# Condition steps moved into the experts' second product, low weight halves made two tiles ahead, and further reorderings in a two-block transformer kernel

## The chip, the cores and the metric

The kernel runs on one core of one Trainium2 chip. The metric is device time in microseconds: 1697.27 us is the median of three runs of the kernel before (1693.96 to 1698.69). The profile is of one further execution.

## The reference, cut to what matters

One sequence of 256 positions with 1024 channels, all in float32, goes through two blocks. The first has an attention layer of two kinds side by side, then a layer of 16384 experts. The second has two layers, each a mixer and a gated feed-forward; the vectors that scale and shift its norms come from a condition `c` through a large product, here called the condition product.

```python
# first block
h = rms_norm(x, attn_norm)
sb_q, sb_k, sb_v, cq, ckv, k_pe = split(h @ w_in)
sb  = stick_breaking_attention(sb_q, sb_k, sb_v)              # 8 heads of 64
q   = rms_norm(rms_norm(cq, cq_norm) @ w_uq, q_norm)          # then rope on 32 of 96
kv  = rms_norm(ckv, ckv_norm) @ w_ukv                         # keys and values
k   = rms_norm(concat(k_nope, k_pe), k_norm)                  # then rope
mla = chunk_causal_softmax_attention(q, k, v)
x   = x + concat(rms_norm(sb), rms_norm(mla)) @ w_o
x   = x + peer_ffn(rms_norm(x))          # sum over chosen experts of g * gelu(x.u) * v
# second block: shift, scale and gate come from silu(c) @ ada
layer 0: x += g * (concat(rmsnorm(diff_attend(..)), fourier(..)) @ w_out); x += g * swiglu(..)
layer 1: x += g * conformer(..)   # product, 31-tap depthwise conv, layernorm, silu, product
         x += g * swiglu(..)      # (silu(h @ w1) * (h @ w3)) @ w2, width 2816
```

## The kernel before, in words

Every weight is used as a high and a low half in a reduced float format, and three products (high by high, high by low of the activations, low by high) stand for one float32 product. A weight tile is 128 by 1024 numbers and costs TensorE 24 matmuls of 256 columns. `_load` issues its DMA on SyncE, `_hi` makes the high half on ScalarE (a tile called `wh`), `_lo` the low half on VectorE (`a<-a,wh`). `next_w` (L629) hands out tile i: it loads into a ring of four raw slots as earlier tiles are given back, then emits `_hi` up to tile i+2 and `_lo` up to tile i+`los`. All engines take their instructions in the order in which they were emitted, so the place of an `_hi` or `_lo` in its engine's row of work says what it waits behind.

The first mixer makes the queries and the compressed keys, then four value tiles (`for i in range(4)`, L896) between which it writes the normalised `cq` (`wq`) and `ckv` (`wk`) and runs steps of `rope`, which builds the sine and cosine tables. After this the key's rope is applied, and a planner (`weave`) mixes the main line of products (`main`, steps `s`: a query and a key tile, `k`: keys, `v`: values, `m`: queries of the second kind) with the tasks of the attention heads.

The experts' second product (L1368) is a loop over 128 keys, one weight tile each. Between the tiles the condition product advances by steps of `ada`, a VectorE pass over a 128 by 1024 tile with an accumulated sum: three steps in every five keys for layer 0. The 48 steps of layer 1 are taken later, in the differential mixer (`diff`) and in the feed-forward of layer 0.

`diff` mixes six heads and a Fourier part, whose results form eight tiles that are multiplied by the output weight in the order `ORDER`. Each feed-forward (`ffn`, L1720) is a loop over 22 slices f: a tile of w1, a tile of w3, and the w2 tile of the slice before. `Pre` lets its first `raws` tiles use the activations before normalisation, with the scale applied afterwards (`praw`, `pcol` on VectorE), while `pre.write()` writes the normalised ones. In the layer-0 feed-forward each f also takes two `ada` steps and builds four diagonal matrices for the convolution on ScalarE.

The conformer convolves with taps divided over TensorE (`PE_TAPS`), GpSimd (`POOL_TAPS`) and VectorE; then come the sums for the layer norm, the Silu, and the last product.

Of the kernel before, what the change touches and what calls it, by code (L numbers as in the profile page):

```python
# [2 lines left out]

# [12 lines left out]
AF = mybir.ActivationFunctionType  # L16
# [4 lines left out]
P = 128  # L21
# [16 lines left out]
PE_TAPS = (8, 9, 9, 9, 9, 9, 14, 15)  # L38
# [35 lines left out]
ORDER = (6, 0, 1, 2, 3, 7, 4, 5)  # L74
# [372 lines left out]
class Net:  # L447
# [394 lines left out]
    def first_mixer(self, ctx):  # L842
# [49 lines left out]
        next(wq)  # L892
# [20 lines left out]
        self.copy(kr[64:QR], kpe[64:QR], scale=self.vec("k_norm")[64:QR])  # L913
        for o, i in ((slice(64, 80), slice(96, QR)), (slice(96, QR), slice(64, 80))):
            nc.vector.tensor_tensor(kt[o], kr[i], self.sinE[i], op=ALU.mult)
        nc.vector.tensor_tensor(kr[64:QR], kr[64:QR], self.cosE[64:QR], op=ALU.mult)
        for o in (slice(64, 80), slice(96, QR)):
            nc.vector.tensor_tensor(kr[o], kr[o], kt[o], op=ALU.add)
# [16 lines left out]

        def main():
# [233 lines left out]
    def peer(self, ctx):  # L1170
# [186 lines left out]
        cg = None  # L1357
        for i in range(NKEYS):
# [18 lines left out]
            if i == 6:  # L1377
                for v in range(2):
                    self.act(cs[v], cs[v], AF.Silu)
                self.table(AF.Exp)  # L1380
                ada = self.ada(0, [self.t(sp, [P, D], tag=f"adaw{i}") for i in range(2)], cs, self.arena(0, D))
            if i > 8 and i % 5 < 3:
                next(ada, None)
# [13 lines left out]
    def ada(self, layer, ws, cs, junk=None):  # L1397

        nc = self.nc
        at = 0  # L1400

        def load():
            nonlocal at
            if at < 48:
                nc.sync.dma_start(ws[at % len(ws)], self.a["ada"][layer, at])
                at += 1
# [4 lines left out]
        for m in range(48):  # L1411
# [41 lines left out]
    def diff(self, ctx):  # L1453
# [13 lines left out]
        self.steps = self.ada(1, [ar(14 * U + i * D, D) for i in range(3)], [ar(5120, D)])  # L1467
# [95 lines left out]
        def main():  # L1563
# [61 lines left out]
        self.pre = Pre(self, self.xT, *self.modulation(2, 0, 1), 0, ar(12 * U, 3, 2, T), ar(12 * U + 1536, T), ar(8 * U, KD, T), AF.Silu, 6)  # L1625
# [92 lines left out]
    def ffn(self, ctx, layer):  # L1718
# [4 lines left out]
        self.los = 1  # L1723
        acc = [self.bank("at") for _ in range(4)]
        cs = []
        for f in range(NF + 1):
# [24 lines left out]
            for _ in range((2, 3, 0, 0)[min(f, 3)]):  # L1751
                pre.write()
# [29 lines left out]
    def conformer(self, ctx):  # L1782
# [22 lines left out]
        def conv_pool(j):  # L1805
            p, u, n = taps[j % 2], us[j % 3], POOL_TAPS[j]
            for i in range(n):
                k = TAPS - n + i
                kw = {"bias": self.vec("dw_b", j)} if i == 0 else {}
                nc.scalar.activation(p[:, i], u[:, k:k + T], AF.Identity if i == 0 else AF.Copy, scale=dw(j, k), **kw)  # L1810
            while n > 1:
# [108 lines left out]
        nc.gpsimd.tensor_tensor(pt[j], pt[j], c, op=ALU.subtract)  # L1920
# [4 lines left out]
        while self.w_lo < self.w_used + 2:  # L1925
            self._lo()
# [5 lines left out]
        self.copy(d, sums[0], scale=1.0 / D)  # L1932
# [4 lines left out]
        for k in range(2):  # L1937
            nc.vector.tensor_tensor(y[:, k], y[:, k], dp, op=ALU.subtract)
        for k in range(2, KD, 2):
            nc.gpsimd.tensor_tensor(y[:, k], y[:, k], d, op=ALU.subtract)  # L1940

        def normal(k):
            if k > 1 and k % 2 == 1:
# [11 lines left out]
        for k in range(KD):  # L1955
            if k < KD - 2:
                self.acc_t(acc, self.next_w(), hh[:, k], hl[:, k], k == 0)
            if k == KD // 2:
                self.table(AF.Exp)
                self.pre = Pre(self, self.xT, *self.modulation(4, 1, 1), 0, ar(13 * U, 3, 2, T), ar(13 * U + 1536, T), ar(7 * U, KD, T), AF.Silu, 6)  # L1960
# [195 lines left out]
```

## Time and profile before

| | us |
|---|---|
| median of the runs | 1697.27 |
| the profiled execution | 1694.07 |
| its span | 1692.3 |
| TensorE busy | 1636.0 (97%) |
| VectorE busy | 1333.6 (79%) |
| ScalarE busy | 1009.4 (60%) |
| GpSimd busy | 325.5 (19%) |

In the profile PE is TensorE, DVE VectorE, ACT ScalarE, POOL GpSimd and SP SyncE. Almost all PE rows have one line number and almost all others another, since helpers record them; so groups are told apart by the names of their tiles and by their time.

### The profile page before, as it was taken

The numbers are of one execution on the slowest core, as the hardware profiler recorded it, in microseconds if no ns is written. First come the engines' busy times: TensorE is split into PE (matmuls) and PEld (weight loads), VectorE is DVE, ScalarE is ACT, GpSimd is POOL, SyncE is SP. The second block draws the span as 40 slices with busy tenths as digits, with TensorE's granted clock in tenths as the row PEclk, the third lists the DMA queues.
The fourth block names the chain that finished last, engine by engine and source line by source line (L and its number), as shares of the span: only waits on it lengthen the run. The fifth ranks groups of instructions, "written<-read, shape, count | busy, mean of one in ns | idle before, by whom it ended". The sixth has DMA issues, their size and how long they took to land.

```text
span 1692.3 us, 33577 instructions
## 1 busy us (share of the span) xinstructions
PE 1636.0 (97%) x12986; PEld 1574.0 (93%) x12986; DVE 1333.6 (79%) x2379; ACT 1009.4 (60%) x1935; POOL 325.5 (19%) x198
## 2 busy tenths in 40 slices
PE   7999999999999999999999999998999989899998
PEld 6878999999999999999999997878999989789997
DVE  7787999977778867878788789976877799885555
ACT  5875554578777756444454564565655677564444
POOL 1020789900000000000000024311000057310000
PEclk9999999999999999999999999999999999999999
DMA  7323455544444456677887753323888732245553
GB/s 218 117 88 120 157 178 180 180 161 162 163 164 162 162 197 233 236 248 235 320 291 275 249 195 119 133 100 123 306 305 300 257 113 100 75 152 187 186 187 125
DMA packets 88110, 315.66 MB, mean 187 GB/s; under 512 B 10000, under 2 KB 11024, under 8 KB 87696
## 3 DMA queue, kind: packets, MB, share of 16 engines
q1 hardware_dynamic: 87952, 313.51, 54.7%
q8 instruction: 104, 1.70, 0.4%
q14 instruction: 54, 0.44, 0.1%
HBM read 312.03 MB, written 1.05 MB: 185 GB/s over the span
## 4 chain that ended last, share of the span: by engine, by line
PE 71%; DVE 14%; ACT 6%; DMA 4%; POOL 2%; issue 2%; SPq 0%; DVEq 0%; ACTq 0%; POOLq 0%
PE mm L179 41%; PE at L179 30%; DVE a L209 10%; ACT a L209 3%; POOL a L209 2%; DMA a<-in_peer_v_dram 2%; ACT wh L209 2%; DMA a<-in_w_dram 1%; DMA a<-in_peer_u_dram 1%; DVE praw L209 1%; DVE dmx L209 1%; DVE xT L209 1%; DVE adaw L209 0%; DVE gb L209 0%; DVE de L209 0%
## 5 line engine op out<-in xcount | busy, mean ns | idle before, releaser
L209 ACT ACTIVATE wh<-a 128x1024 fp32r<-128x1024 f32 (+3 forms) x491 | 515.1, 1053 | 262.6 <-DMA a<-in_w_dram 120.4
L179 PE MATMUL mm<-a,wh 128*128 128x256 f32 (+3 forms) x4736 | 655.1, 287 | 13.5 <-ACT wh L209 6.8
L209 DVE TENSOR_TENSOR a<-a,wh 128x1024 fp32r<-128x1024 f32 (+2 forms) x436 | 533.3, 1230 | 121.3 <-ACT wh L209 115.9
L179 PEld LDWEIGHTS mm<-a,wh 128*128 128x128 f32 (+1 forms) x4736 | 600.7, 189 | 26.6 <-ACT wh L209 7.6
L179 PE MATMUL mm<-a,a 128*128 128x256 f32 (+5 forms) x2608 | 409.3, 295 | 12.3 <-DVE a L209 7.9
L179 PEld LDWEIGHTS mm<-a,a 128*128 128x128 f32 (+1 forms) x2608 | 354.6, 190 | 24.0 <-DVE a L209 6.5
L179 PE MATMUL at<-a,wh 128*128 128x256 f32 x2152 | 283.3, 282 | 7.3 <-DVE a L209 4.9
L179 PEld LDWEIGHTS at<-a,wh 128*128 128x128 f32 x2152 | 268.5, 190 | 9.3 <-DVE a L209 5.7
L209 POOL TENSOR_TENSOR a<-a 128x256 f32<-128x256 f32 (+4 forms) x44 | 71.5, 1626 | 885.5 <-ACT a L209 860.0
L179 PE MATMUL at<-a,a 128*128 128x256 f32 (+6 forms) x1288 | 210.5, 297 | 2.3 <-DVE a L209 2.3
L179 PEld LDWEIGHTS at<-a,a 128*128 128x128 f32 (+2 forms) x1288 | 171.5, 190 | 16.6 <-issue 10.5
L209 ACT ACTIVATE a<-a 128x256 fp32r<-128x256 f32 (+7 forms) x220 | 99.1, 460 | 109.2 <-DVE a L209 87.1
L209 POOL TENSOR_TENSOR a<-a,a 128x256 f32<-128x256 f32 (+5 forms) x62 | 80.3, 1300 | 427.6 <-ACT a L209 336.4
L209 POOL TENSOR_TENSOR a<-a,wh 128x1024 fp32r<-128x1024 f32 x54 | 147.1, 2745 | 17.1 <-ACT wh L209 16.8
L209 DVE TENSOR_TENSOR a<-a,a 128x256 fp32r<-128x256 f32 (+7 forms) x189 | 111.7, 592 | 22.3 <-ACT a L209 17.5
L209 ACT ACTIVATE a<-mm 128x256 f32<-128x256 f32 (+29 forms) x173 | 60.2, 352 | 95.8 <-PE mm L179 95.7
L179 PE MATMUL at<-fgh,wh 128*128 128x256 f32 x352 | 86.3, 282 | 2.2 <-ACT wh L209 2.2
L179 PE MATMUL at<-fgl,wh 128*128 128x256 f32 x352 | 86.1, 282 | 0.0
L209 ACT ACTIVATE oh<-oh,rest 128x128 f16<-128x128 f16 x256 | 81.1, 398 | 0.0
L209 DVE TENSOR_TENSOR fs<-fs,mm 128x256 f32<-128x256 f32 x38 | 16.0, 422 | 76.3 <-PE mm L179 76.3
L209 DVE TENSOR_TENSOR a<-a,at 128x204 f32<-128x204 f32 (+54 forms) x115 | 36.6, 355 | 48.7 <-PE at L179 41.8
L179 PEld LDWEIGHTS at<-fgh,wh 128*128 128x128 f32 x352 | 66.4, 189 | 2.7 <-ACT wh L209 2.7
(163 smaller groups left out, 1565.4 us busy)
## 6 DMA issues: line engine op xcount, KB each, us to landing
a<-in_w_dram SPq DMA_DIRECT2D x132, 512.0 KB, 3.5
a<-in_peer_u_dram SPq DMA_DIRECT2D x128, 512.0 KB, 3.3
a<-in_peer_v_dram SPq DMA_DIRECT2D x128, 512.0 KB, 4.0
adaw<-in_ada_dram SPq DMA_DIRECT2D x48, 512.0 KB, 4.4
a<-in_ada_dram SPq DMA_DIRECT2D x48, 512.0 KB, 4.9
a<-in_pw_dram SPq DMA_DIRECT2D x24, 512.0 KB, 3.3
a<-in_w_pq_dram SPq DMA_DIRECT2D x16, 512.0 KB, 3.2
a<-in_ev_qkf_dram SPq DMA_DIRECT2D x14, 512.0 KB, 3.6
```

Of the source, the lines that this page charges most:

```text
L179: return self.engine.matmul(out, w, x, **kw)
L209: return f(*args, **kw)
```

## The change

There are five places.

In the first mixer `ckv` is written before `cq`, the table steps run one per value tile, and the rest of them with the key's rope (`key_rope`) goes into the first `qk` of the main line; the DMA that spreads the rotated key to all heads moves to the `k` step. In `diff` the tile order changes and eight `ada` steps go away. They are taken in the experts' second product, which now does 1.03 steps per key for 32 keys and 0.515 per key after. In both feed-forward layers `raws` goes from 6 to 10, `pre.write()` is spread one per slice, and `los` goes from 1 to 2. In the conformer one tap moves from TensorE to VectorE, one subtraction on GpSimd moves ahead of the tree sum, and the work around the layer norm is reordered: one `_lo` ahead and one behind instead of two ahead.

```diff
-PE_TAPS = (8, 9, 9, 9, 9, 9, 14, 15)
+PE_TAPS = (8, 9, 9, 9, 9, 9, 14, 14)
-ORDER = (6, 0, 1, 2, 3, 7, 4, 5)
+ORDER = (6, 7, 0, 1, 2, 3, 4, 5)
+FIRSTMODS = 8
@@ first mixer
-        next(wq)
         nk.mm()
...
-                if kk == 0:
-                    next(rope, None)
-            next(wq, None)
-            next(wk, None)
+            if i < 2:
+                next(wk, None)
+            if i > 0:
+                next(wq, None)
             next(rope, None)
-        for _ in rope:
-            pass
...
+        def key_rope():
+            for _ in rope:
+                yield
+            self.copy(kr[64:QR], kpe[64:QR], scale=self.vec("k_norm")[64:QR])
...
                 if kind == "s":
-                    yield from qk(p)
-                    if p == 0:
-                        nc.sync.dma_start(km[64:QR], self.bc(kr[64:QR], HEADS))
+                    for _ in qk(p):
+                        if p == 0:
+                            next(turned, None)
+                        yield
...
                 if kind == "k":
+                    for _ in turned:
+                        pass
+                    nc.sync.dma_start(km[64:QR], self.bc(kr[64:QR], HEADS))
@@ the experts' second product
-            if i > 8 and i % 5 < 3:
-                next(ada, None)
+            if i > 8:
+                while given < 1.03 * min(i - 8, 32) + 0.515 * max(i - 40, 0):
+                    next(ada, None)
+                    given += 1
@@ diff
-        self.steps = self.ada(1, [ar(14 * U + i * D, D) for i in range(3)], [ar(5120, D)])
+        self.steps = self.ada(1, [ar(14 * U + i * D, D) for i in range(3)], [ar(5120, D)], begin=FIRSTMODS)
...
-            for n, _ in enumerate(values(1, "mm")):
-                if 1 < n < 7:
-                    next(steps, None)
-                yield
+            yield from values(1, "mm")
             for i in range(2):
                 self.copy(fT[:, i], self.tile_t(lh, ll))
-                next(steps, None)
                 yield
-            next(steps, None)
...
-        self.pre = Pre(self, self.xT, *self.modulation(2, 0, 1), 0, ar(12 * U, 3, 2, T), ar(12 * U + 1536, T), ar(8 * U, KD, T), AF.Silu, 6)
+        self.pre = Pre(self, self.xT, *self.modulation(2, 0, 1), 0, ar(12 * U, 3, 2, T), ar(12 * U + 1536, T), ar(8 * U, KD, T), AF.Silu, 10)
@@ ffn
-        self.los = 1
+        self.los = 2
...
-            for _ in range((2, 3, 0, 0)[min(f, 3)]):
+            if f < 5:
                 pre.write()
@@ conformer
-        nc.gpsimd.tensor_tensor(pt[j], pt[j], c, op=ALU.subtract)
...
-        while self.w_lo < self.w_used + 2:
-            self._lo()
+        self._lo()
...
-        for k in range(2):
-            nc.vector.tensor_tensor(y[:, k], y[:, k], dp, op=ALU.subtract)
-        for k in range(2, KD, 2):
-            nc.gpsimd.tensor_tensor(y[:, k], y[:, k], d, op=ALU.subtract)
+        nc.vector.tensor_tensor(y[:, 0], y[:, 0], dp, op=ALU.subtract)
+        self._lo()
```

How the instructions move is shown at three places. The first is ScalarE in the first mixer, behind the fourth value tile. `wh` is a weight's high half; the 32-row instructions are the sines; `a_98<-at` are the two copies of the values. Before:

```order
L209 ACTIVATE wh_446<-a_81 128x1024
L209 ACTIVATE a_156<-a_152 128x64
L209 ACT_TABLE_LOAD
L209 ACTIVATE a_104<-a_152 32x64
L209 ACTIVATE a_103<-a_156,a_159 32x64
L209 ACTIVATE a_104<-a_152 32x64
L209 ACTIVATE a_103<-a_156,a_159 32x64
L209 ACTIVATE wh_471<-a_86 128x1024
```

And in the changed kernel, where `wh_482` is the first key tile, `wh_520` the next one, and `a_105` the last piece of `cq`:

```order
L211 ACTIVATE a_105<-a_95 128x256
L211 ACTIVATE a_156<-a_152 128x64
L211 ACT_TABLE_LOAD
L211 ACTIVATE wh_482<-a_90 128x1024
L211 ACTIVATE a_104<-a_152 32x64
L211 ACTIVATE a_103<-a_156,a_159 32x64
L211 ACTIVATE a_104<-a_152 32x64
L211 ACTIVATE a_103<-a_156,a_159 32x64
L211 ACTIVATE a_98<-at_399 128x512
L211 ACTIVATE a_98<-at_400 128x512
L211 ACTIVATE wh_520<-a_77 128x1024
```

The last piece of `cq`, which before stood ahead of the fourth value tile, now stands with the table load ahead of the first key tile's high half.

The second is VectorE in the layer-0 feed-forward, from the low half of the first activations on (`fgl`). `praw` and `pcol` take a raw tile's result out of its bank, `a<-a,wh` is a weight's low half. Before:

```order
L209 TENSOR_TENSOR fgl_13811<-fs_13803,fgh_13810 128x256
L209 SCALAR_TENSOR_TENSOR a_114<-xT,modA,a_13579 128x256 x4
L209 SCALAR_TENSOR_TENSOR a_66<-a_114,mods,a_65 128x256 x2
L209 TENSOR_TENSOR praw_13853<-mm_13828,a_13579 128x256
L209 COPY pcol_13854<-mm_13828 128x1
L209 TENSOR_TENSOR a_222<-a_86,wh_13826 128x1024
L209 TENSOR_TENSOR praw_13888<-mm_13863,a_13579 128x256
L209 COPY pcol_13889<-mm_13863 128x1
```

In the changed kernel:

```order
L211 TENSOR_TENSOR fgl_13810<-fs_13802,fgh_13809 128x256
L211 SCALAR_TENSOR_TENSOR a_114<-xT,modA,a_13579 128x256 x2
L211 TENSOR_TENSOR a_222<-a_86,wh_13819 128x1024
L211 TENSOR_TENSOR praw_13847<-mm_13822,a_13579 128x256
L211 COPY pcol_13848<-mm_13822 128x1
L211 TENSOR_TENSOR a_226<-a_90,wh_13854 128x1024
L211 TENSOR_TENSOR praw_13882<-mm_13857,a_13579 128x256
L211 COPY pcol_13883<-mm_13857 128x1
```

A low half now stands ahead of each `praw`, where one stood behind it.

The third is ScalarE at the end of `diff`. `a<-at,eps` is the logarithm in the norm of the last head, and the two rows after it finish that norm; `wh` are the first two weights of the feed-forward. Before:

```order
L209 ACTIVATE wh_13541<-a_90 128x1024
L209 ACTIVATE a_12056<-at_13547 128x256
L209 ACTIVATE a_13559<-a_12056 128x256
L209 ACTIVATE a_13559<-at_13567,eps 128x256
L209 ACTIVATE a_13559<-a_13559 128x256
```

In the changed kernel:

```order
L211 ACTIVATE a_65<-a_12073 128x256
L211 ACTIVATE a_13542<-a_12073 128x256
L211 ACTIVATE wh_13547<-a_86 128x1024
L211 ACTIVATE wh_13551<-a_90 128x1024
L211 ACTIVATE a_13542<-at_13544,eps 128x256
L211 ACTIVATE a_13542<-a_13542 128x256
```

Two high halves now stand between the square and the logarithm of the last head.

## Rows read from the trace of the kernel before

**Rows 1.** The page: span, then busy time and share of each engine.

```profile
span 1692.3 us, 33577 instructions
...
PE 1636.0 (97%) x12986; PEld 1574.0 (93%) x12986; DVE 1333.6 (79%) x2379; ACT 1009.4 (60%) x1935; POOL 325.5 (19%) x198
```

**Rows 2.** The page: the chain that ended last, by engine.

```profile
PE 71%; DVE 14%; ACT 6%; DMA 4%; POOL 2%; issue 2%; SPq 0%; DVEq 0%; ACTq 0%; POOLq 0%
```

**Rows 3.** TensorE's waits, whole span: us in total, times, longest.

```profile
PE mm L179 <- DVE a L209: 10.6, 14, 2.0
...
PE at L179 <- DVE se L209: 0.4, 1, 0.4
```

**Rows 4.** Windows, first mixer: us, busy of PE, PEld, DVE, ACT, POOL; clock, DMA, GB/s.

```profile
40.00:46.00 6.00, 2.23 (x6) 1.52 (x7) 4.77 (x15) 4.17 (x9) 0.77 (x1) 0.73 0.24 87
46.00:60.00 14.00, 14.00 (x94) 12.82 (x92) 10.37 (x17) 11.70 (x20) 0.00 (x0) 0.87 0.44 117
```

**Rows 5.** Timeline of PE, fourth value tile: start, us, operation [idle before, releaser].

```profile
41.92 0.73 PE L179 MATMUL at<-wh,a 128*128 128x512 f32 x2 [2.71 <-ACT wh L209]
44.50 0.80 PE L179 MATMUL at<-a,a 128*128 128x512 f32 x1 [1.85 <-DVE a L209]
```

**Rows 6.** Timeline of ACT, same place.

```profile
40.29 0.63 ACT L209 ACTIVATE a<-a 128x512 fp32r<-128x512 f32 x1 [0.71 <-DVE a L209]
...
43.62 1.28 ACT L209 ACT_TABLE_LOAD   x1
44.91 0.26 ACT L209 ACTIVATE a<-a 32x64 f32<-32x64 f32 x1
...
50.93 1.09 ACT L209 ACTIVATE a<-at 128x512 f32<-128x512 f32 x2
```

**Rows 7.** Timeline of DVE, same place.

```profile
43.22 1.22 DVE L209 TENSOR_TENSOR a<-a,wh 128x1024 fp32r<-128x1024 f32 x1
...
51.67 2.20 DVE L209 TENSOR_TENSOR a<-a,a 16x256 f32<-16x256 f32 x5
```

**Rows 8.** Lines of ACT, 60 to 160 us: busy, mean ns, idle before, releasers.

```profile
L209 ACT ACTIVATE se<-se 128x384 f32<-128x384 f32 x22 | 11.4, 520 | 5.3 <-DVE se L209 4.8
```

**Rows 9.** Timeline of PE, the experts' second product, two keys.

```profile
703.04 2.05 PE L179 MATMUL at<-a,wh 128*128 128x256 f32 x16
...
705.87 2.05 PE L179 MATMUL at<-a,wh 128*128 128x256 f32 x16
```

**Rows 10.** Timeline of DVE, the same product, two keys with a condition step each.

```profile
910.89 1.21 DVE L209 SCALAR_TENSOR_TENSOR adaw<-adaw,cs 128x1024 f32<-128x1024 f32 x1
...
913.50 1.21 DVE L209 SCALAR_TENSOR_TENSOR adaw<-adaw,cs 128x1024 f32<-128x1024 f32 x1
```

**Rows 11.** TensorE's waits, 800 to 950 us.

```profile
PE at L179 <- ACT wh L209: 2.1, 4, 1.0
```

**Rows 12.** Timeline of PE, end of the differential mixer.

```profile
1153.08 0.70 PE L179 MATMUL at<-a,cons 128*128 128x256 f32 x2 [2.60 <-ACT a L209]
...
1155.76 1.47 PE L179 MATMUL mm<-a,wh 128*128 128x256 f32 x4 [1.74 <-ACT a L209]
```

**Rows 13.** Timeline of ACT, same place.

```profile
1151.26 1.06 ACT L209 ACTIVATE wh<-a 128x1024 fp32r<-128x1024 f32 x1 [3.23 <-DMA a<-in_w_dram]
```

**Rows 14.** Timeline of PE, start of the layer-0 feed-forward.

```profile
1177.43 0.39 PE L179 MATMUL at<-fgh,wh 128*128 128x256 f32 x1 [1.12 <-ACT wh L209]
...
1185.85 1.23 PE L179 MATMUL mm<-a,a 128*128 128x258 f32 x8 [0.49 <-DVE a L209]
```

**Rows 15.** Timeline of DVE, same place: a condition step.

```profile
1188.37 1.22 DVE L209 SCALAR_TENSOR_TENSOR a<-a,a 128x1024 f32<-128x1024 f32 x1
```

**Rows 16.** Timeline of ACT, same place: four diagonal matrices.

```profile
1188.91 1.27 ACT L209 ACTIVATE a<-cons,vecs 128x128 f32<-128x128 f32 x4
```

**Rows 17.** Timeline of DVE, conformer layer norm: the two low halves.

```profile
1454.44 2.35 DVE L209 TENSOR_TENSOR a<-a,wh 128x1024 fp32r<-128x1024 f32 x2
```

**Rows 18.** Timeline of PE, same place.

```profile
1460.37 4.03 PE L179 MATMUL at<-a,wh 128*128 128x256 f32 x16 [4.64 <-DVE a L209]
```

More of the change, by code (lines that the diff above doesn't have):

```diff
@@ L2 @@
 from contextlib import ExitStack
+from itertools import chain
 import numpy as np
@@ L903, in first_mixer @@
                     self.mm3_n(pv[g], hh[:, k, ts], hl[:, k, ts], wh[:, ws], wl[:, ws], k == 0, k == KD - 1)
-                if kk == 0:
-                    next(rope, None)
-            next(wq, None)
-            next(wk, None)
+            if i < 2:
+                next(wk, None)
+            if i > 0:
+                next(wq, None)
             next(rope, None)
-        for _ in rope:
-            pass
         self.los = 1
         kr, kt = ar(0, T), ar(T, T)
[L913 to L918, printed above, removed]
+        def key_rope():
+            for _ in rope:
+                yield
+            self.copy(kr[64:QR], kpe[64:QR], scale=self.vec("k_norm")[64:QR])
+            for o, i in ((slice(64, 80), slice(96, QR)), (slice(96, QR), slice(64, 80))):
+                nc.vector.tensor_tensor(kt[o], kr[i], self.sinE[i], op=ALU.mult)
+            nc.vector.tensor_tensor(kr[64:QR], kr[64:QR], self.cosE[64:QR], op=ALU.mult)
+            yield
+            for o in (slice(64, 80), slice(96, QR)):
+                nc.vector.tensor_tensor(kr[o], kr[o], kt[o], op=ALU.add)
+            yield
         done = Done(self.pe)
@@ L934, in qk @@
                 yield
+        turned = key_rope()
         def main():
@@ L941, in main @@
                 if kind == "s":
-                    yield from qk(p)
-                    if p == 0:
-                        nc.sync.dma_start(km[64:QR], self.bc(kr[64:QR], HEADS))
+                    for _ in qk(p):
+                        if p == 0:
+                            next(turned, None)
+                        yield
                     continue
@@ L1356, in peer @@
         tile_u(NKEYS - 1)
-        cg = None
+        cg, given = None, 0
         for i in range(NKEYS):
@@ L1380, in peer @@
                 self.table(AF.Exp)
-                ada = self.ada(0, [self.t(sp, [P, D], tag=f"adaw{i}") for i in range(2)], cs, self.arena(0, D))
-            if i > 8 and i % 5 < 3:
-                next(ada, None)
+                ws = [self.t(sp, [P, D], tag=f"adaw{i}") for i in range(2)]
+                ada = chain(self.ada(0, ws, cs, self.arena(0, D)), self.ada(1, ws, cs, end=FIRSTMODS))
+            if i > 8:
+                while given < 1.03 * min(i - 8, 32) + 0.515 * max(i - 40, 0):
+                    next(ada, None)
+                    given += 1
             if i == 64:
@@ L1393, in peer, with ada @@
             self.pre.pair(k)
-    def ada(self, layer, ws, cs, junk=None):
+    def ada(self, layer, ws, cs, junk=None, begin=0, end=48):
         nc = self.nc
-        at = 0
+        at = begin
         def load():
             nonlocal at
-            if at < 48:
+            if at < end:
                 nc.sync.dma_start(ws[at % len(ws)], self.a["ada"][layer, at])
@@ L1410, in ada @@
         yield
-        for m in range(48):
+        for m in range(begin, end):
             load()
@@ L1810, in conv_pool @@
                 nc.scalar.activation(p[:, i], u[:, k:k + T], AF.Identity if i == 0 else AF.Copy, scale=dw(j, k), **kw)
+                if i == 0 and j == KD - 1:
+                    nc.gpsimd.tensor_tensor(p[:, 0], p[:, 0], c, op=ALU.subtract)
             while n > 1:
@@ L1931, in conformer @@
         self.copy(dp, sums[0], scale=1.0 / D)
-        self.copy(d, sums[0], scale=1.0 / D)
         nc.vector.scalar_tensor_tensor(r, sums[1], 1.0 / D, d2, op0=ALU.mult, op1=ALU.subtract)
@@ L1936, in conformer @@
         self.table(AF.Silu)
-        for k in range(2):
-            nc.vector.tensor_tensor(y[:, k], y[:, k], dp, op=ALU.subtract)
-        for k in range(2, KD, 2):
-            nc.gpsimd.tensor_tensor(y[:, k], y[:, k], d, op=ALU.subtract)
+        nc.vector.tensor_tensor(y[:, 0], y[:, 0], dp, op=ALU.subtract)
+        self._lo()
         def normal(k):
-            if k > 1 and k % 2 == 1:
+            if k == 1:
+                self.copy(d, sums[0], scale=1.0 / D)
+                for i in range(2, KD, 2):
+                    nc.gpsimd.tensor_tensor(y[:, i], y[:, i], d, op=ALU.subtract)
+            if k % 2 == 1:
                 nc.vector.tensor_tensor(y[:, k], y[:, k], dp, op=ALU.subtract)
@@ L1959, in conformer @@
                 self.table(AF.Exp)
-                self.pre = Pre(self, self.xT, *self.modulation(4, 1, 1), 0, ar(13 * U, 3, 2, T), ar(13 * U + 1536, T), ar(7 * U, KD, T), AF.Silu, 6)
+                self.pre = Pre(self, self.xT, *self.modulation(4, 1, 1), 0, ar(13 * U, 3, 2, T), ar(13 * U + 1536, T), ar(7 * U, KD, T), AF.Silu, 10)
         self.acc_last(acc, [(hh[:, k], hl[:, k]) for k in (KD - 2, KD - 1)])
```

## The prediction

> **What bounds the kernel now.** I read the page first. TensorE is busy in 1636.0 of 1692.3 us [rows 1], so 56.3 us of the span are not its work, and the chain that ended last is TensorE for 71%, VectorE for 14% and ScalarE for 6% [rows 2]. Then the list of TensorE's waits: eleven kinds, of which the first and the last are shown, add up to 47.6 us [rows 3]. The change takes no product away, except a tap of the convolution, so all it can win lies in those 47.6 us and in what the lowered clock behind a wait costs. The rest was read by place, in the timelines of TensorE, ScalarE and VectorE.
>
> The engines take work in order. A high half is a ScalarE pass of about 1.06 us [rows 13], a low half a VectorE pass of 1.22 us when alone and 1.14 us from one to the next [rows 7, 17]; a tile's 24 matmuls take 705.87 - 703.04 = 2.83 us [rows 9]. TensorE waits wherever a half stands in its engine's row behind something that itself waits. The question at each place is what a half stands behind now.
>
> **First mixer.** Today the fourth value tile waits 2.71 us for its high half and 1.85 us for its low half [rows 5], since on ScalarE a copy of `cq` stands ahead that waits for VectorE [rows 6]. The granted clock is 0.73 of full speed around it and 0.87 in the 14 us after, its lower level (1.2 GHz) for part of both [rows 4]: 2.23 x 0.27 + 14.00 x 0.13 = 2.4 us. So 4.56 + 2.4 = 7.0 us can go. With the late pieces of `cq` behind the fourth tile's halves, that tile's wait goes whole. What is late next are the tiles behind it. I walked the new order with the durations of these rows. The low half of the first query tile ends on VectorE near 43.7 and the last piece of `cq` near 44.1. ScalarE then copies it, makes one small pass, loads the sine table in 1.28 us [rows 6] and makes the first key tile's high half, which ends near 47.1, where TensorE arrives at about 44.6: a wait of 2.5. The next weight's low half stands behind two VectorE passes that need the last sines. These end on ScalarE near 51.5, because the value copies (1.09) and a high half come between [rows 6]; the low half is there near 53.2, TensorE at about 51.0: 2.2. The low half of the `ukv` value tile stands behind the five passes of the key's rope, 2.20 us [rows 7], which start after a second table load and the key copy: 1.9. With 0.2 at the first query tile that is 6.8 us, and the clock falls again behind it as it does today. So 6.8 - 4.56 = +2.2 for the waits, but the sine and key work that today comes behind these tiles is then done, and the planner fills some of it; I take 0. Bounds: -7.0 if none of the three comes, +3 if all do and none is filled.
>
> A row here bears on a rule. The instruction behind the sine table's load starts at 44.91, 0.01 us after the load's end (43.62 + 1.28) [rows 6]. The Trainium skill (ScalarE: Activation LUTs, What ACT_TABLE_LOAD costs) puts a drain of about 1.38 us beside the 1.28 us of a load, 2.66 us a switch. By that rule the two loads, which now stand ahead of halves, would cost 2 x 1.38 = 2.8 us more than I count, an estimate from that page; the trace shows no such gap.
>
> **Attention behind it.** In the new order seven or eight groups of the stick-breaking attention stand together ahead of the second attention's norm, and the output weights behind them in one run of 96 matmuls, where today they alternate. A group has ScalarE passes of 0.52 us, and these waited 4.8 us for VectorE in this stretch already [rows 8]. If the chain of the last groups is left bare, two rounds of some 2 us are added: +4; if the planner's filler suffices, 0. I take +1, nearer to the row's side where waits are spread over 22 passes.
>
> **Experts' second product.** A key is 2.83 us on TensorE [rows 9], and a key with one condition step takes VectorE 913.50 - 910.89 = 2.61 us [rows 10]. Today's steps come in threes and in some keys two passes stand behind each other; now the rate is 1.03 per key, then about half. 2.61 + 0.03 x 1.14 = 2.65 us a key is 94% of 2.83, so it fits. What may go are the waits of 2.1 us for a high half [rows 11], as the transfers are spread evenly too: I take -1.3, with -2.1 and +4 as ends. The +4 is for 32 keys that each run late by 0.13 us, with a step in each. The eight steps cost nothing here while VectorE stays under TensorE's 2.83; without that cover they cost 8 x 1.14 = 9.1.
>
> **Differential mixer.** It loses eight VectorE passes of 1.14 us and their transfers. At its end TensorE waits 2.60 and 1.74 us today [rows 12], because a high half that waited 3.23 us for its DMA stands ahead of the last head's norm [rows 13]. In the new order two high halves stand there, the weight slots of which come free only as TensorE ends earlier output tiles. DMA, two copies, and the logarithm, exponent and multiply behind them give about 4.5 + 1.05 + 1.9 = 7.5 us, of which 2.4 are covered by matmuls: 5.1 instead of 4.34, +0.7. Elsewhere in the stage VectorE has less to do; a wait of about 1.2 goes. Sum -0.5, ends -4 (both waits gone) and +2.
>
> **Feed-forward of layer 0.** Today it waits 1.12 and 0.49 us at its start [rows 14]. The low half for the tile after next now stands ahead of each `praw`, and it needs a high half that stands on ScalarE behind passes that need VectorE, which need `praw` of the tile before. There are two such turns in each slice, and in the slices from the third on, 2 x 1.22 us of condition steps [rows 15] and 1.27 us of diagonal matrices [rows 16] lie between them. One slice is 3 x 2.83 = 8.5 us of TensorE. On VectorE it is three low halves (3.4), two condition steps (2.3) and ten short passes of the order shown, between 0.1 and 0.4 each (2.8 by the walk): 8.5, no slack at all; on ScalarE three high halves (3.2), the matrices (1.3) and the short passes (1.7): 6.2. With their turns the walk gives 11.3, a wait of up to 2.8 a slice, part of which the tiles made ahead cover. The bounds for the three late raw slices (f = 2, 3, 4, of which the last two are raw only now): -1.6 (today's waits go, none comes) and 3 x 2.8 - 0.8 = +7.6. The nearest row is the 1.12 wait of one such turn; one in each of three slices, less 0.8 won at the start, is +2.5. The walk over all three, with what is covered, comes to +4.6. I take +3.5, between them. The layer-1 feed-forward has the same order without steps and matrices, so about 3 us less a slice on the two engines: -0.2, ends -1.6 and +1.
>
> **Conformer.** TensorE waits 4.64 us before the last product [rows 18]. Two low halves, 2.35 us, stand in VectorE ahead of the variance [rows 17]; one now moves behind the Silu's input, so the chain should shorten by about 1.14, and the earlier subtraction gives a little more, less one tap on VectorE of about 0.4. I take -1.4, ends -2 and 0.
>
> **Sum.** 0 + 1 - 1.3 - 0.5 + 3.5 - 0.2 - 1.4 = +1.1 us on the profiled execution's 1694.07. That execution stands 3.2 us under the median of 1697.27; on the median that is 1698.4, which I predict. The difference that a measurement can tell from none is 0.3%, 5.1 us: under 1692.2 is faster, over 1702.4 slower. The ends of the terms, taken as independent (half their widths 5.0, 2.0, 3.0, 3.0, 4.6, 1.3, 1.0, squared and added, and the root), give 8.4 us.
>
> **Rivals.** *The waits go and nothing takes their place.* The mixer gives its 7.0, the experts 1.3, the differential mixer 0.5, the feed-forward layers their 1.6 and 0.2, the conformer 1.4, less 1 for the attention: -11.0, 1686.3; with half the mixer's gain 1690. For it speaks that before waits were short wherever a half was made far ahead; against it that the new order puts a table load and a VectorE wait ahead of high halves that have no slack.
>
> *The feed-forward's turns at full price.* ScalarE and VectorE wait for each other in f = 2 to 4 of layer 0, +7.6 instead of +3.5: 1698.4 + 4.1 = 1702.5, slower. With the attention's +4 as well it is 1705.5. It decides from the point where a slice takes the two engines over 8.5 us. For it speaks VectorE's 8.5 us a slice without any turn; against it that two tiles are made ahead before the run of raw tiles ends, and that a tile ahead is 2.83 us of cover.
>
> *The experts' keys don't fit.* If 32 keys take VectorE 0.13 us too long each, +4 instead of -1.3: 1703.7. The 0.18 us between 2.65 and 2.83 speak against it.
>
> *The table's drain counts*, as the rule above has it: with the drain where no gap is now, +2.8: 1701.2. The row speaks against it.
>
> **How the numbers follow.** My forecast has 0.45, the waits that go 0.28, the feed-forward's turns 0.19, the keys 0.05, the drain 0.03. Within 0.3% are 0.37 of the forecast, the drain, and the edges of the two large rivals: 0.43. Faster: most of the first rival and 0.04 of the forecast, 0.30; slower: the turns, the keys and 0.04 of the forecast, 0.27. The likeliest case alone reaches from 1692 to 1704; the range over all is 1687 to 1706.
>
> **What would show it.** In the changed profile the wait of 2.71 at the fourth value tile is gone, and waits of about 2 stand at the first key tile, the next one and the `ukv` tile, with the granted clock under 1 up to 60 us. A key of the experts' product stays at 2.83. The last wait of `diff` is about 5. In layer 0's feed-forward TensorE waits for VectorE's or ScalarE's halves between the fifth and tenth raw tile, some 4 us in all. The conformer's wait is near 3.2. It is wrong if the mixer shows no such waits, if the feed-forward runs without waits or with over 2 us a slice, or if the waits of TensorE in sum differ from 47.6 by over 5.

## The result, and the profile after

The changed kernel takes 1725.24 us (median; 1722.06 to 1734.79) against 1697.32 for the kernel before: a ratio of 1.0175, 95% interval 1.0156 to 1.0194. It is 28 us slower, outside the range that was given, and the likeliest case was no change.

The page of the changed kernel, to be held against [rows 1, 2]:

```profile
span 1720.2 us, 33550 instructions
...
PE 1646.7 (96%) x12984; PEld 1578.5 (92%) x12984; DVE 1340.3 (78%) x2396; ACT 1010.8 (59%) x1934; POOL 320.4 (19%) x198
...
PE 71%; DVE 10%; ACT 8%; DMA 5%; issue 4%; POOL 2%; SPq 0%; DVEq 0%; ACTq 0%; POOLq 0%
```

The work is the same: TensorE has two instructions fewer of 12986. Its waits have changed kind. These are the largest of the list, beside [rows 3] (us in total, times, longest):

```profile
PE mm L181 <- DVE a L211: 18.2, 16, 3.4
PE mm L181 <- ACT wh L211: 14.3, 13, 5.7
PE at L181 <- ACT wh L211: 13.5, 21, 2.2
```

and these are the waits for high halves (`wh`) before:

```profile
PE at L179 <- ACT wh L209: 7.3, 8, 2.7
PE mm L179 <- ACT wh L209: 6.8, 3, 5.7
```

Waits for high halves were 7.3 and 6.8 us and are 13.5 and 14.3; waits of `mm` for VectorE were 10.6 and are 18.2. All waits of the list add up to 64.5 us where they were 47.6; the other 10.7 of the 28 us are busy time of TensorE, 1646.7 where 1636.0 stood. Where the time went is best seen by stages. A stage ends here at the start of a matmul that both traces have, and the table gives its length in the profiled execution of the kernel before, and what that of the changed kernel adds to it, in us:

| stage | before | changed | as forecast |
|---|---|---|---|
| first mixer, to its residual | 155.8 | +4.9 | +1.0 |
| to the experts' second product | 461.9 | -1.3 | 0 |
| experts' second product | 367.7 | +10.1 | -1.3 |
| differential mixer | 175.6 | -4.7 | -0.5 |
| feed-forward 0, to its fifth w2 tile | 51.5 | +10.5 | +3.5 |
| feed-forward 0, the rest | 143.0 | +4.6 | 0 |
| conformer | 130.9 | +0.3 | -1.4 |
| feed-forward 1 | 197.5 | +3.5 | -0.2 |

The sum is 27.9 us, as in the medians. Three quarters of it lie in the two stages that the prediction put down as "it fits" and "+3.5".

**Experts' second product.** The timeline of TensorE, two keys, beside [rows 9]:

```profile
674.41 2.16 PE L181 MATMUL at<-a,wh 128*128 128x256 f32 x16 [0.56 <-ACT wh L211]
...
677.37 2.05 PE L181 MATMUL at<-a,wh 128*128 128x256 f32 x16
...
680.91 2.16 PE L181 MATMUL at<-a,wh 128*128 128x256 f32 x16 [0.55 <-ACT wh L211]
```

680.91 - 674.41 = 6.50 us for two keys, where two keys took 5.66. This repeats from 668 to 754 us and then stops. The timeline of VectorE over one such pair, beside [rows 10]:

```profile
673.44 0.43 DVE L211 TENSOR_TENSOR a<-a,a 128x256 fp32r<-128x256 f32 x1 [0.57 <-ACT a L211]
674.39 1.23 DVE L211 TENSOR_TENSOR a<-a,wh 128x1024 fp32r<-128x1024 f32 x1 [0.52 <-ACT wh L211]
675.53 1.22 DVE L211 SCALAR_TENSOR_TENSOR adaw<-adaw,cs 128x1024 f32<-128x1024 f32 x1
...
677.01 1.22 DVE L211 TENSOR_TENSOR a<-a,wh 128x1024 fp32r<-128x1024 f32 x1
678.15 1.22 DVE L211 SCALAR_TENSOR_TENSOR a<-adaw,cs 128x1024 f32<-128x1024 f32 x1
...
679.94 0.43 DVE L211 TENSOR_TENSOR a<-a,a 128x256 fp32r<-128x256 f32 x1 [0.57 <-ACT a L211]
```

The passes come as counted, 2.6 us a key. But behind each pass whose product goes to `a` (the pass of 678.15) VectorE waits twice, 0.57 for ScalarE's copy of a coefficient and 0.52 for a high half. Two keys of work take 2 x 2.62 = 5.24 us; with these 1.09, and 0.17 at the rows ahead of the waits, whose last part no longer overlaps a next row, it is 6.5. The copy itself waits, too:

```profile
679.49 0.42 ACT L211 ACTIVATE a<-a 128x256 fp32r<-128x256 f32 x1 [3.15 <-PE at L181]
```

The profile names TensorE here, but the copy starts 0.12 us behind the end of that pass (678.15 + 1.22 = 679.37), and so do all fourteen copies that wait behind such a pass between 660 and 760 us. Why a copy of a coefficient should wait for the pass is not to be seen here; the third and the second experiment tell.

**Feed-forward 0.** TensorE at the third and the fourth w2 tile and at the first tile behind the raw ones, beside [rows 14]:

```profile
1206.06 0.39 PE L181 MATMUL at<-fgh,wh 128*128 128x256 f32 x1 [2.19 <-ACT wh L211]
...
1217.53 0.39 PE L181 MATMUL at<-fgh,wh 128*128 128x256 f32 x1 [1.07 <-ACT wh L211]
...
1226.30 0.63 PE L181 MATMUL mm<-a,wh 128*128 128x256 f32 x3 [3.39 <-DVE a L211]
```

This raw slice takes 1217.53 - 1206.06 = 11.5 us. ScalarE and VectorE in it, first ScalarE:

```profile
1204.97 1.04 ACT L211 ACTIVATE wh<-a 128x1024 fp32r<-128x1024 f32 x1
1207.76 0.51 ACT L211 ACTIVATE fs<-praw,pcol 128x256 f32<-128x256 f32 x1 [1.75 <-DVE pcol L211]
1208.17 2.00 ACT L211 ACTIVATE wh<-a 128x1024 fp32r<-128x1024 f32 x2
```

and VectorE:

```profile
1206.04 1.22 DVE L211 TENSOR_TENSOR a<-a,wh 128x1024 fp32r<-128x1024 f32 x1 [1.15 <-ACT wh L211]
1207.18 0.42 DVE L211 TENSOR_TENSOR praw<-mm,a 128x256 f32<-128x256 f32 x1
...
1209.25 1.22 DVE L211 TENSOR_TENSOR a<-a,wh 128x1024 fp32r<-128x1024 f32 x1 [1.58 <-ACT wh L211]
```

Each engine's wait ends on the other: ScalarE's Silu (`fs`) waits for `pcol`, which stands behind a low half, which waited for ScalarE's high half; the next high half stands behind that Silu.

### The profile page after: what moved, and what is told of

It reads as the page before. It is cut to its first block, busy times and chain, and to the rows that moved or that the text cites. A ratio compares the mean times of both kernels' runs of the same rounds, so it can differ in the third digit from the quotient of the medians.

```text
span 1720.2 us, 33550 instructions
## 1 busy us (share of the span) xinstructions
PE 1646.7 (96%) x12984; PEld 1578.5 (92%) x12984; DVE 1340.3 (78%) x2396; ACT 1010.8 (59%) x1934; POOL 320.4 (19%) x198
## 4 chain that ended last, share of the span: by engine, by line
PE 71%; DVE 10%; ACT 8%; DMA 5%; issue 4%; POOL 2%; SPq 0%; DVEq 0%; ACTq 0%; POOLq 0%
PE mm L181 40%; PE at L181 30%; DVE a L211 8%; ACT a L211 3%; ACT wh L211 3%; DMA a<-in_w_dram 2%; POOL a L211 2%; DMA a<-in_peer_v_dram 1%; ACT L211 1%; DMA a<-in_peer_u_dram 1%; DVE xT L211 1%; DVE praw L211 0%; PE at L186 0%; DVE gb L211 0%; DVE mx L211 0%
## 5 line engine op out<-in xcount | busy, mean ns | idle before, releaser
L181 PE MATMUL mm<-a,wh 128*128 128x256 f32 (+3 forms) x4736 | 660.3, 289 | 27.8 <-ACT wh L211 14.3
L181 PEld LDWEIGHTS at<-a,a 128*128 128x128 f32 (+2 forms) x1288 | 171.0, 189 | 14.5 <-issue 10.9
L211 ACT ACTIVATE a<-a 128x256 fp32r<-128x256 f32 (+9 forms) x220 | 98.8, 459 | 116.1 <-DVE a L211 56.7
L211 DVE TENSOR_TENSOR a<-a,a 128x256 fp32r<-128x256 f32 (+7 forms) x189 | 112.0, 593 | 29.7 <-ACT a L211 26.2
L211 DVE SCALAR_TENSOR_TENSOR adaw<-adaw,cs 128x1024 f32<-128x1024 f32 x56 | 70.4, 1258 | 0.1
```

The lines of the kernel that those rows point to most:

```text
L181: return self.engine.matmul(out, w, x, **kw)
L211: return f(*args, **kw)
```

## The experiments

Times are medians in us; the ratio is to the kernel before, run beside it on the same chip. Stage numbers are made as in the table above, from each run's profiled execution. How far one execution can be trusted is seen where programs have the same code in a stage: with the changed code the experts' second product reads +8.9 to +11.3, feed-forward 0 +10.4 to +11.0 up to its fifth w2 tile and +4.2 to +6.9 behind it, feed-forward 1 +3.3 to +5.2. For five runs (even rate, six raw tiles, one load ahead, start of the mixer, tile order) the interval of the ratio overlaps that of the changed kernel, so their medians alone tell nothing; the stages do.

**Even rate of condition steps.** Edit on the changed kernel:

```diff
-                while given < 1.03 * min(i - 8, 32) + 0.515 * max(i - 40, 0):
+                while given < 0.64 * (i - 8):
```

Expected: 

> Changed kernel, but the condition steps of the experts' second product come at an even 0.64 per key over all its keys (same 72 steps in all) where the changed kernel gives 1.03 per key for 32 keys and then half that. Both theories of the slow keys (the transfer queue held by a condition tile's load that waits for VectorE; VectorE itself full with a pass in each key) expect the product to lose its regular waits: 32 keys of 3.25 us go back to 2.83, -9 to -12 us, about 1714 us. If the time stays above 1720, the rate is not the cause.

Measured: 1723.23, ratio 1.0147 (1.0129 to 1.0164). Neither theory's number. The product still costs 9.6 us more than before. The waits of the first 32 keys are gone, but 800 to 960 us has new ones, 6.7 us for high halves, where the changed kernel has none. SyncE's waits in that stretch, this kernel and then the changed one:

```profile
SPq L1419 <- DVE a L211: 75.9, 28, 6.5
```

```profile
SPq L1419 <- DVE a L211: 10.6, 15, 3.0
```

By the rule set ahead, a time above 1720 would clear the rate; the stage shows two effects. The rate of 1.03 harms while a tile takes two passes; once a tile takes one pass, 0.515 is harmless and 0.64 holds SyncE's queue, since a step in the next key then loads into the tile that the key before has just used. This second effect is read from the waits; no run took it alone.

**Three tiles for the condition loads.** Edit on the changed kernel (the steps begin four keys later):

```diff
+        def buffer(m):
+            if third is None:
+                return ws[m % len(ws)]
+            return (ws + [third])[m % 3] if m < 15 else ws[(m - 15) % 2]
...
-                ada = chain(self.ada(0, ws, cs, self.arena(0, D)), self.ada(1, ws, cs, end=FIRSTMODS))
+                ada = chain(self.ada(0, ws, cs, self.arena(0, D), third=self.arena(4 * T, D)), self.ada(1, ws, cs, end=FIRSTMODS))
```

Expected: 

> Changed kernel with 1.03 condition steps per key kept (begun 4 keys later), but three tiles for the loads of the condition product where there were two, for the 15 tiles that take two passes each. A load then waits for a pass that is two keys older. Theory 'queue': the load no longer holds SyncE's queue, weights land on time, the waits for high halves in this product go, -7 to -11 us, about 1715 us. Rival 'VectorE full': a pass in each key is unchanged, keys stay at about 3.2 us, 1724 us.

Measured: 1740.69, ratio 1.0266 (1.0249 to 1.0283), 15 us worse than the changed kernel, against both theories. The third tile lay in memory that the first coefficient tiles had left. The timeline of ScalarE shows what a coefficient copy waits for now:

```profile
697.40 0.42 ACT L211 ACTIVATE a<-a 128x256 fp32r<-128x256 f32 x1 [5.24 <-DMA a<-in_ada_dram]
```

A copy of a coefficient waits for a condition tile's load, with which it has no number in common. It reads another part of the same memory (the arena that holds all coefficients); the load writes into that arena. Over 660 to 800 us these waits are 26.2 us in five. The unread product of the two-pass tiles (`junk`) has lain in the same place all along. That is a third theory, which the next run tests by itself.

**The unread product apart.** Edit on the changed kernel:

```diff
-                ada = chain(self.ada(0, ws, cs, self.arena(0, D)), self.ada(1, ws, cs, end=FIRSTMODS))
+                ada = chain(self.ada(0, ws, cs, self.t(sp, [P, D], F16, tag="junk")), self.ada(1, ws, cs, end=FIRSTMODS))
```

Expected: 

> Changed kernel, but a condition pass's product that nobody reads (one of the two passes of a tile writes it) goes to a 16-bit tile of its own, not to the memory of the first coefficient tiles. Theory 'false wait': ScalarE's copy of a later coefficient reads the same region, so it waits for that pass, VectorE then waits for the copy, and two keys take 6.5 us; with the tile apart ScalarE's copies no longer wait for VectorE, keys of the first 32 go to 2.83 us, -8 to -11 us, about 1714 us. Rival 'queue' (a condition load that waits for VectorE holds the weights' loads): keys stay at 3.25 us, 1723 to 1726 us. Rival 'VectorE full': the same as 'queue', with VectorE busy without a gap.

Measured: 1714.54, ratio 1.0105 (1.0084 to 1.0126): 10.7 us back. The product takes 0.3 us less than before. VectorE's timeline over one key, with the same passes:

```profile
676.24 1.22 DVE L211 SCALAR_TENSOR_TENSOR adaw<-adaw,cs 128x1024 f32<-128x1024 f32 x1
...
677.38 0.42 DVE L211 TENSOR_TENSOR a<-a,a 128x256 fp32r<-128x256 f32 x1
677.72 1.22 DVE L211 TENSOR_TENSOR a<-a,wh 128x1024 fp32r<-128x1024 f32 x1
678.86 1.22 DVE L211 SCALAR_TENSOR_TENSOR junk<-adaw,cs 128x1024 f16<-128x1024 f32 x1
```

A key is 678.86 - 676.24 = 2.62 us without a gap. TensorE's waits for high halves over 660 to 760 us, the changed kernel and then this one:

```profile
PE at L181 <- ACT wh L211: 8.8, 15, 0.8
```

```profile
PE at L181 <- ACT wh L211: 1.7, 3, 1.1
```

SyncE still waits 69.6 us for VectorE in that stretch, so in the two-pass keys the held queue alone costs little, and VectorE was not full. One thing came otherwise than expected: ScalarE's copies still wait for VectorE.

```profile
ACT a L211 <- DVE a L211: 24.9, 21, 1.7
```

But each of these 21 ends 0.09 us behind the low half of the coefficient before, and none behind a condition pass, where the changed kernel has fourteen copies, 43.8 us in all, that start 0.12 us behind one. Beside its place only the type of the unread product was edited, and its pass takes 1.22 us as before. So the false wait is shown: the copy needs nothing that this pass makes, waited for it while both lay in the arena, and that cost the 10 us.

**The same edit on the kernel before.**

```diff
-                ada = self.ada(0, [self.t(sp, [P, D], tag=f"adaw{i}") for i in range(2)], cs, self.arena(0, D))
+                ada = self.ada(0, [self.t(sp, [P, D], tag=f"adaw{i}") for i in range(2)], cs, self.t(sp, [P, D], F16, tag="junk"))
```

Expected: 

> Kernel before with one edit: the unread product of the two-pass condition steps in a 16-bit tile of its own. In the kernel before two keys of five have no pass and VectorE catches up there, so theory 'false wait' expects almost nothing: -2 to 0 us, 1695 to 1697. If the false wait cost something in each of the 16 tiles there too, -4 us or more.

Measured: 1697.98, ratio 0.9999 (0.9990 to 1.0008). The false wait was there before and cost nothing that a median shows. That the two keys in five without a pass paid for it is the likely reason; no run took it alone. By stages this program, whose time is the same, reads +1.4, +0.1, +2.0, +1.6, 0, +0.7, +0.3 and 0 in the order of the table: a difference of up to 2 us in one stage of one profile means nothing by itself.

**Feed-forward layers as before.** The three edits undone (`los` 1, `raws` 6, writes of two and three). Expected: 

> Changed kernel with the three edits of both feed-forward layers undone (low halves one tile ahead, six raw tiles, two and three writes in the first slices). Theory 'turns' (ScalarE and VectorE wait for each other in the raw slices): layer 0 gives back 12 us of its raw slices, and layer 1 some 5: about 1708 us. If the last 5 us of layer 0 (slices 13 to 20, high halves waiting for transfers) come from the same edits, 1703 us. Rival: the feed-forward layers are slow because what comes ahead of them is late, then above 1720.

Measured: 1707.25, ratio 1.0069 (1.0052 to 1.0085), 18 us back. Layer 0 takes 0.3 us less than before and layer 1 0.3 less, so both the raw slices and the late ones come from these edits.

**Low halves one tile ahead, the other two edits kept.**

```diff
         steps = self.steps
-        self.los = 2
+        self.los = 1
```

Expected: 

> Changed kernel with one of the three feed-forward edits undone: low halves one tile ahead, while ten raw tiles and one write per slice stay. If the low halves' place ahead of the raw results makes the turns, most goes: slices of 8.5 us where 11.5 stand now, -6 to -12 us, 1713 to 1719; a wait of some 3 us at the first tile after the raw ones stays in both layers. If the longer run of raw tiles is the cause by itself (its passes fill VectorE), the slices stay at 10 us or more and the time above 1720.

Measured: 1706.95, ratio 1.0055 (1.0033 to 1.0077). The whole loss goes, more than expected, and the wait of 3.39 at the first tile behind the raw ones with it (the longest that is left is 0.6). Layer 0 is within 0.6 us of before, layer 1 takes 1.6 us less. So the loss needs the low halves two ahead. Ten raw tiles gain 1.6 us in layer 1, here and in the joined kernel below, and nothing in layer 0.

**Six raw tiles, low halves two ahead.** Expected: 

> Changed kernel with the raw tiles back at six and the writes back at two and three in the first slices, while low halves stay two tiles ahead. If the place of the low halves alone makes the turns, slices f = 2 and 3 of layer 0 stay near 11.5 us where they are raw and the late 5 us of slices 13 to 20 stay: 1714 to 1719. If both edits are needed, below 1710. The late 5 us separate: they stay if they come from low halves two ahead (a condition pass behind the newest low half, and its load holding the queue).

Measured: 1721.44, ratio 1.0141 (1.0123 to 1.0159). Only 3.8 us back, less than expected: layer 0 still takes 14.1 us more, but 10.8 of it lie behind its fifth w2 tile and 3.3 ahead of it, where the changed kernel has 10.5. Its slices up to there take 10.7, 9.1, 9.4 and 9.2 us, none of them the 11.5 that the place of the low halves alone was to give. So two ahead is bad by itself, above all in the late slices; the 11.5 us slices need the ten raw tiles as well.

**The condition load one tile ahead.** Edit on the changed kernel, for the three tiles of layer 1's steps:

```diff
-        for _ in range(len(ws) - 1):
+        for _ in range(1):
             load()
```

Expected: 

> Changed kernel, but of the three tiles for the condition loads of layer 1 the load runs one tile ahead and not two, so that it waits for an older pass. Theory 'queue' for the late slices of the layer-0 feed-forward (loads of weights stand behind a condition load that waits for VectorE): SyncE's wait for VectorE there falls from 78 to under 20 us, slices 13 to 20 run at 8.51 us, -4 to -6 us, about 1720. If the late slices are slow for another reason, 1725. The raw slices (turns of ScalarE and VectorE) should keep most of their 11.5 us in either case.

Measured: 1723.12, ratio 1.0155 (1.0138 to 1.0173). SyncE's largest wait over 1236 to 1390 us, the changed kernel and then this one:

```profile
SPq L1419 <- DVE a L211: 76.4, 26, 6.0
```

```profile
SPq L602 <- PE mm L181: 79.3, 35, 4.4
```

The queue waits for a free weight slot again, as it should; its wait for VectorE at a condition load is 2.8 us. The slices behind the fifth run at 8.51 us: that stretch goes from +4.6 to -1.0 us against before, and the raw slices stay at +11.0. The median gives only 2.1 us, less than the stage. The first mixer of this program's profiled execution ends 4.0 us later than that of the changed kernel, though its code is the same; the nine programs with the changed mixer scatter from +4.9 to +8.9 there.

**Start of the first mixer as before.** Expected: 

> Changed kernel with the start of the first mixer as before (cq written first, table steps and key rope ahead of the main line). Theory: the attention's groups, standing together without filler, cost the 4 to 6 us that the changed kernel loses up to the end of the first mixer: 1719 to 1721. Rival: the loss there is scatter between programs, then 1724 to 1726.

Measured: 1721.75, ratio 1.0146 (1.0127 to 1.0164). 3.5 us back; its mixer ends at +0.4, and in two more kernels with the old start at +1.2 and +1.4, against +4.9 to +8.9 with the changed one. The changed start is a loss.

**Tile order of the differential mixer as before.** Expected: 

> Changed kernel with the order of the eight output tiles of the differential mixer as before. The changed kernel wins some 5 us in that mixer. If the eight condition steps that left it are the reason, it keeps 4 to 5 of these: 1724 to 1727. If the tile order is, it loses them: 1728 to 1731.

Measured: 1727.53, ratio 1.0178 (1.0157 to 1.0199). That mixer keeps 4.4 of its 4.7 us: the tile order is worth nothing that shows. With the feed-forward edits undone it keeps 5.7. What is left of the edits there is the eight steps that went away, so the gain is put down to them by exclusion; no run put them back.

**Joined.** The changed kernel with the old mixer start, the unread product apart, and `los` 1 in the feed-forward layers. Expected: 

> Changed kernel with three things put right: the start of the first mixer as before, the unread product in a 16-bit tile of its own, and low halves one tile ahead in the feed-forward layers (ten raw tiles and one write per slice stay). Kept: eight condition steps in the experts' product, the differential mixer without them, the conformer's edits. By the stages of the runs so far: mixer 0, experts' product 0 to -2, differential mixer -4 to -5, feed-forward 0 and -1.6, conformer 0 to +1: 1688 to 1692 us, faster than the kernel before. If the gain of the differential mixer was only an effect of its late start, 1696.

Measured: 1686.87, ratio 0.9936 (0.9922 to 0.9950), faster than both kernels, 11 us under the one before. Its page:

```profile
span 1685.6 us, 33576 instructions
...
PE 1633.7 (97%) x12984; PEld 1572.2 (93%) x12984; DVE 1332.8 (79%) x2396; ACT 1012.5 (60%) x1934; POOL 328.1 (19%) x198
```

By stages: mixer +1.2, experts' product -0.3, differential mixer -5.9, feed-forward 0 within 0.1, feed-forward 1 -1.6. So what the change was right in is the eight steps moved and, in layer 1, the ten raw tiles. These stages add up to some -6.5 us, as the two profiled executions do (1687.42 against 1694.07); that of the kernel before lies 4.2 us under the median beside it, and in which stage the rest of the 11 us lies is not known.

## Why the prediction was wrong

Two steps of the sum failed: "it fits" for the experts' second product (-1.3 forecast, +10.1 measured), and the size of the turns in feed-forward 0 (+3.5 forecast, +10.5 measured, and +4.6 behind them where nothing was put). The waits in sum, which were to stay within 5 us of 47.6, are 64.5.

**Experts' second product: the step failed in kind.** It counted VectorE's passes, 2.65 us a key of 2.83, and called it a fit. The rival "the keys don't fit" had the right place, but VectorE's own time as the reason, and +4. Adding up one engine's work assumes that it never waits for another. The rows for the 2.61 us of a key [rows 10] came from 910 us, where a tile takes one pass. The added steps went where a tile takes two, and the trace of before shows VectorE there, too:

```profile
679.90 1.22 DVE L209 TENSOR_TENSOR a<-a,wh 128x1024 fp32r<-128x1024 f32 x1
681.03 1.22 DVE L209 SCALAR_TENSOR_TENSOR a<-adaw,cs 128x1024 f32<-128x1024 f32 x1
...
682.83 0.43 DVE L209 TENSOR_TENSOR a<-a,a 128x256 fp32r<-128x256 f32 x1 [0.57 <-ACT a L209]
683.78 1.23 DVE L209 TENSOR_TENSOR a<-a,wh 128x1024 fp32r<-128x1024 f32 x1 [0.53 <-ACT wh L209]
```

From low half to low half this key takes 683.78 - 679.90 = 3.88 us, not 2.61, with the same two waits as in the changed kernel. ScalarE's waits over 660 to 760 us show the other end of it:

```profile
ACT a L209 <- DVE a L209: 32.0, 14, 3.9
```

Ten of these fourteen waits, 30.0 us, end 0.12 us behind a pass of the unread product; the other four, 2.0 us, behind the low half of a coefficient, as those that stay with the product apart. The dependence was there before, and cost nothing that a median shows. The runs with the unread product apart and with a third tile show it from both sides.

**Feed-forward 0: the mechanism was right, its size cut too far.** The walk over the order gave 11.3 us a slice. The prediction then took +3.5, between the walk with its cover and the row of one 1.12 us wait. That row came from a slice with the low half behind `praw`, another order; it was no bound for the new one, and the cover did not show. The three slices take 11.9, 11.5 and 14.5 us where 8.5 stood, the last with the wait of 3.39 at the first tile behind the raw ones, for the last of the writes (1225.76 + 0.48 on VectorE), which stands behind the turns: 12.4 us more, less 1.8 won ahead of them, make +10.5, outside the +7.6 that was the upper end. Part of this is the clock, for which the sum had a term in the first mixer and none here: behind the waits of 2.19 and 3.39 it falls to its lower level (1.2 GHz) for a time. The granted clock is 0.90 over 1198 to 1215 us, with 14.81 us busy, and 0.88 over 1226 to 1240, with 13.70, so an estimate by the prediction's own way of counting is 14.81 x 0.10 + 13.70 x 0.12 = 3.1 us. The late slices were not thought of: what stands behind a condition load on SyncE was not asked. With low halves two ahead a condition pass stands behind a newer weight, its load waits with it, and the weights stand behind the load.

**Feed-forward 1** was put at -0.2, since it has no steps and matrices. It measured +3.5; the turns need neither. The slices up to the tile behind the raw ones take 9.1, 9.6, 9.2 and 11.9 us where 9.5 and then 8.5 stood, the last with a wait of 2.25 for VectorE at that tile. With the low halves one ahead it is -1.6.

**First mixer.** The walk of its start was right in the main: the fourth value tile's waits [rows 5] are gone, and in their place TensorE has

```profile
44.20 1.22 PE L181 MATMUL mm<-a,a 128*128 128x256 f32 x8 [0.43 <-DVE a L211]
47.56 2.16 PE L181 MATMUL mm<-a,wh 128*128 128x256 f32 x16 [2.14 <-ACT wh L211]
...
53.41 0.80 PE L181 MATMUL mm<-a,a 128*128 128x256 f32 x2 [1.89 <-DVE a L211]
...
58.59 0.50 PE L181 MATMUL mm<-a,a 128*128 128x512 f32 x1 [0.64 <-DVE a L211]
```

Forecast were 0.2, 2.5, 2.2 and 1.9 us, 6.8 in all; these are 5.1. The stretch nets +0.5 us, which one profile can't tell from 0. The attention behind it was put at +1, with +4 as the end; it costs 4.4 here and up to 7.1 in the eight other programs with the changed start, while all four programs with the old start take the same 94.1 to 94.2 us for it. The windows of 100 to 120 and 120 to 140 us show TensorE's busy time (second number), before:

```profile
100.00:120.00 20.00, 18.51 (x122) 13.62 (x120) 15.21 (x48) 12.90 (x39) 0.25 (x1) 1.00 0.31 107
120.00:140.00 20.00, 18.98 (x137) 16.82 (x138) 16.74 (x29) 14.59 (x28) 1.03 (x1) 1.00 0.25 79
```

and changed:

```profile
100.00:120.00 20.00, 17.09 (x103) 12.32 (x102) 17.40 (x57) 14.12 (x44) 0.00 (x0) 1.00 0.30 107
120.00:140.00 20.00, 18.07 (x120) 14.19 (x118) 14.15 (x30) 15.74 (x32) 2.57 (x2) 1.00 0.03 7
```

The same 40 us hold 223 matmuls where 259 stood, and TensorE is busy 2.3 us less. That the groups, now without filler between them, are the reason fits the forecast; the run with the old start undid the whole start at once, so it does not show this part alone.

**Differential mixer.** Forecast -0.5, measured -4.7. Its last wait was forecast near 5 and is 2.63, with 0.87 ahead of it, beside [rows 12]:

```profile
1159.07 0.70 PE L181 MATMUL at<-a,cons 128*128 128x256 f32 x2 [0.87 <-ACT a L211]
...
1164.51 1.08 PE L181 MATMUL mm<-a,wh 128*128 128x256 f32 x4 [2.63 <-ACT a L211]
```

The second of the two high halves waited 1.66 us for its load, not the 3.23 of [rows 13], and the wait ahead of it is 0.87 where 2.60 stood. That VectorE, with eight passes less, brought the norm early is argued, not shown.

**Conformer.** The wait of [rows 18] was to shrink to 3.2 and is 4.34, and two shorter ones came behind it:

```profile
1483.73 0.58 PE L181 MATMUL at<-a,wh 128*128 128x256 f32 x1 [4.34 <-DVE a L211]
1484.76 3.57 PE L181 MATMUL at<-a,wh 128*128 128x256 f32 x15 [0.45 <-DVE a L211]
...
1493.63 1.56 PE L181 MATMUL at<-a,wh 128*128 128x256 f32 x11 [0.59 <-ACT wh L211]
```

The layer norm starts the product 0.8 us earlier in its stage and gives 1.1 back. No run took this part alone; the stage reads +0.1 to +0.9 in all runs, among them +0.3 in the one that has the conformer as before, so nothing shows either way.

**The table's drain** did not come, as the row of before said: a high half starts 0.01 and 0.02 us behind the two moved loads (45.16 + 1.28, then 46.45; 52.16 + 1.28, then 53.46), and each load starts 0.02 us behind the pass ahead of it.

## What to carry to other kernels

Ask of every wait in the list of the engine that is not the bottleneck what it waits for and why; a wait without a reason, such as a copy that waits for a pass on other data, may be a false dependence that costs nothing today and that the next change puts on the path. Give unread output memory of its own. Take the row for a sum from the stretch that the change will fill. A load in a queue of loads costs what it waits for, not what it moves: look up when its target comes free, and what stands behind it. Where two engines work by turns, walk the order and trust the walk, to the tile behind its end; rows of another order are no bound for it.

## What had not been expected of the hardware

The pass whose unread product goes to a 16-bit tile takes 1.22 us, as the one with a 32-bit product does. A condition load that waited for VectorE held SyncE's later loads up to 6.5 us in the changed kernel; with the unread product apart, 69.6 us of such waits, up to 6.1 each, stood beside only 1.7 us of TensorE's.
